# Order of the first chunk's exponentials, and place of the first w_o split, in a hybrid pooling and SSD decoder step

## The chip, the core and the metric

The kernel runs on one core of a Trainium2 chip. The core has five instruction queues that run side by side and meet only through semaphores: TensorE (PE, matrix products, its weight loads shown as PEld), VectorE (DVE), ScalarE (ACT), GpSimd (POOL) and SyncE (SP), which issues most of the DMA transfers. ACT issues the rest of them from its own queue, between its computations. Time is the device's time of one execution in microseconds (us); the metric is the median over executions.

## What is computed

One layer of a decoder on 1,024 prompt rows and 64 sample rows, together T = 1,088 columns in the kernel's transposed layout. The parts that matter here:

```
def layer(x, c, pos0, pool_buf, conv_buf, ssm_state, ...):
    h = rmsnorm(x, norm_g) * (1 + scale[:, None]) + shift[:, None]
    proj = h @ w_in
    u_pool, z_pool, z_ssm, xbc, dt_raw, g_raw = jnp.split(proj, SPLITS, axis=-1)
    ...
    p = (p * jax.nn.silu(z_pool)) @ w_pool_out
    ...
    y, ssm_new = ssd(xs, dt, A, Bm, Cm, ssm_state)
    y = rmsnorm(y * jax.nn.silu(z_ssm), ssm_norm_g)
    s = y @ w_ssm_out
    gates = jax.nn.sigmoid(g_raw)
    m = gates[..., :D_MODEL] * p + gates[..., D_MODEL:] * s
    x = x + gate[:, None] * (m @ w_o)

def step(h, inp):                      # inside ssd, one chunk of 128 rows
    acs = jnp.cumsum(dq * Ag, axis=1)
    decay = jnp.exp(jnp.where(mask, acs[:, :, None] - acs[:, None, :], -jnp.inf))
    cb = jnp.einsum('bign,bjgn->bijg', Cq, Bq)
    att = cb[..., None] * decay * dq[:, None]
    ...
```

All of it is float32. A product is made from three passes of a reduced format: each operand is split into a high part `hi` (a rounded copy, made by ACT) and a low part `lo = raw - hi` (a subtraction, made by POOL or DVE), and PE adds up hi·hi, hi·lo and lo·hi.

## The kernel before

The program has three stages that follow one another on PE.

**Projections (to about 827 us).** `h @ w_in` in pairs of column blocks, each by a seven-product scheme (`strassen`, L615). The last ten pairs (`run_units(light[-LAST:], 1, samples_beside)`, L1645) end in a sigmoid: for each half block, DVE adds the last product to a buffer (`s1`, `u2`, `u3`, `c2`; L625), ACT applies the sigmoid in place (`to_dram`, L721), and ACT issues the store to the scratch tensors `gp` and `gs` (L723). Beside each product a function `samples_beside` (L1596) counts steps in `due[0]` and issues other work at fixed steps. Work put under `with behind(engine)` (L406) stands in the scheduler's order right behind the last instruction of that engine written so far.

**Chunks (827 to about 1,124 us).** The SSD runs over 32 chunks (4 groups of 8) in a loop, L1768, with the products of `w_pool_out` and `w_ssm_out` between them (`products`, L1749, which run `gemm`, L354). In this stage the order on all five queues is as written: `in_line` (L340) ties every instruction to the one before it on its engine. For one chunk `i` the pieces are: `ch_load`, `d_load` and `z_load` (loads of `xb`, `dec` and `sz`); `ch_far` (from the second chunk of a group on ACT makes `cE = exp(-dec)`, L1402; then POOL masks `dec`, L1193); `ch_exps` (eight exponentials on ACT in place on `dec`, L1202); `ch_turn` (PE transposes `xb` into the PSUM tiles `pxs` and `pbs`, L118, and multiplies, L1415; ACT copies `bt`, L1417, and C, L1419); `ch_weigh` (DVE `xd`, `ps`, L1426 and L1427; ACT `xw`, L1429); `ch_skip` (ACT `xD`, L1435); `ch_mix` (DVE multiplies `dec`, L1439, and `cE`, L1441); `ch_lows` (DVE `btl`, L1444, and `xwl`, L1445); `ch_inner` (PE, L1214 to L1217 and L1462 to L1464). Chunk 0's `ch_far` and `ch_exps` do not stand in this loop: they are issued from `samples_beside`, at step `7 * LAST - 1`, before the last pair of sigmoids.

**Tail (1,131 us to the end).** Eight units `m` (`tail_unit`, L1898) make the last group's part of `s`, three column blocks each: DVE adds the earlier groups' sum to the product and multiplies by the row gate (L1882 and L1885 for `m = 0`; L1888 and L1890 for the others), POOL adds the pooling branch's part `mt` (L1886, L1892), `m_split` (L1851) makes `hi` on ACT (L1865) and `lo` on DVE (L1866) of the result, and `wo_split` (L1727) makes `hi` on ACT (L1729) and `lo` on POOL (L1730) of one block of 128 rows of `w_o`, which `wo_load` (L1723) has brought in. `m_split(m - 1)` is called in unit `m`. The product's PSUM tiles `mm` rotate over three buffers. The order is again as written on PE, DVE, ACT and POOL, while SP's order is left to the scheduler. At last come the products with `w_o` (L2000 to L2002), the norm and the stores.

Numbers at the end of a tile's name, as in `u_1850`, are those of one program's buffers; the profile leaves them out.

Of the kernel before, what the change touches and what calls it, by code (L numbers as in the profile page):

```python
# [21 lines left out]
D = 1024  # L22
# [24 lines left out]
def tile_pool_ssd_step(  # L47
# [9 lines left out]
    def nm(s):  # L57
        uid[0] += 1
        return f"{s}_{uid[0]}"
# [30 lines left out]
    def R(shape=(P, T), dt=F32):  # L90
        return hs.tile(list(shape), dt, tag="R", name=nm("R"), bufs=3)

    def Y4(pool, dt=F32R):
        return pool.tile([P, 4, T], dt, tag="Y", name=nm("Y"), bufs=2)

    def PB():
        return psB.tile([P, 512], F32, tag="ps", name=nm("ps"))
# [19 lines left out]
    def turn_r(out, src):  # L117
        nc.tensor.transpose(out.bitcast(F32R), src.bitcast(F32R), identR)  # L118
# [221 lines left out]
    def in_line(engines, begin=False):  # L340
        traced = nc.cur_bb.bb.instructions
        for i in traced[len(traced) if begin else line[0]:]:
            if i.engine in engines:
                if i.engine in line[1]:
                    tc.add_manual_dep(i, line[1][i.engine], mybir.DependencyInfo(
                        mybir.DependencyClass.NoSync, mybir.DependencyReason.DATA), reason="in_line")
                line[1][i.engine] = i.name
        line[0] = len(traced)
# [57 lines left out]
    def behind(engine, n=0):  # L406

        of = (i for i in reversed(nc.cur_bb.bb.instructions) if i.engine == engine)
        for _ in range(n):
            next(of)  # L410
        return tc.issue_after(next(of))
# [44 lines left out]
    def ready(d):  # L456
        def ws():
            with tc.high_priority(PRI):
                hi, lo = wtiles()
                load(hi.bitcast(F32), d[:, 0])  # L460
                load(lo.bitcast(F32), d[:, 1])
            return [(hi, lo)]
        return ws
# [726 lines left out]
    def far(dec, c):  # L1190

        if c < NC:
            nc.gpsimd.affine_select(dec, dec, [[0, 8], [1, P]], ALU.is_ge, FAR, base=0, channel_multiplier=-1)  # L1193
        else:
            dS = dec.rearrange("p h (b i) -> p h b i", i=8)
            nc.gpsimd.affine_select(dS, dS, [[0, 8], [8, NB], [1, 8]], ALU.is_ge, FAR, base=0, channel_multiplier=-1)
            nc.gpsimd.affine_select(dS, dS, [[0, 8], [-8, NB], [0, 8]], ALU.is_ge, FAR, base=0, channel_multiplier=1)

    def exps(dec, g, c):
        S = P if c < NC else NS  # L1200
        for h in range(8):
            act(dec[:, h], dec[:, h], AF.Exp, bias=acT[:S, c, 8 * g + h:8 * g + h + 1], scale=-1.0)  # L1202
# [160 lines left out]
    def ckt(shape, tag, bufs=2):  # L1363
        return (cl if tag in CKL else ca if tag in ("dec", "xb", "cE") else ck).tile(list(shape), F32, tag=tag, name=nm(tag), bufs=bufs)
# [19 lines left out]
    def ch_load(i):  # L1384
        g, c = divmod(i, NC)
        xbs[i] = ckt([P, 6, P], "xb", 3)
        load(xbs[i], xbc_d[g][:, :, c * P:c * P + P])

    def d_load(i):
        g, c = divmod(i, NC)  # L1390
        decs[i] = ckt([P, 8, P], "dec", 3)
        decays(decs[i], g, c)

    def z_load(i):
        g, c = divmod(i, NC)
        szs[i] = ckt([P, 4, P], "sz", 3)
        load(szs[i], z_d[g][:, :, c * P:c * P + P])

    def ch_far(i):
        if i % NC > 0:  # L1400
            cEs[i] = ckt([P, 8, P], "cE", 3)
            act(cEs[i], decs[i], AF.Exp, scale=-1.0)  # L1402
        far(decs[i], i % NC)

    def ch_exps(i):
        g, c = divmod(i, NC)
        exps(decs[i], g, c)

    def ch_turn(i):
        xb = xbs[i]  # L1410
        pxs[i], pbs[i] = PB(), PB()
        for q in range(4):
            turn_r(pxs[i][:, q * P:(q + 1) * P], xb[:, q])
        turn_r(pbs[i][:, :P], xb[:, 4])
        mm(pbs[i][:, P:2 * P], xb[:, 4], xb[:, 5], start=True, stop=True)  # L1415
        bts[i] = [ck.tile([P, P], F32R, tag=t, name=nm(t), bufs=2) for t in ("bt", "btl")]
        act(bts[i][0], pbs[i][:, :P], AF.Copy)  # L1417
        if i % NC > 0:
            act(pbs[i][:, 2 * P:3 * P], xb[:, 5], AF.Copy)  # L1419

    def ch_weigh(i):
        g, c = divmod(i, NC)
        heads = slice(8 * g, 8 * g + 8)
        pxv = pxs[i].rearrange("p (h d) -> p h d", d=64)
        xds[i] = ckt([P, 8, 64], "xd", 2)
        V.tensor_tensor(xds[i], pxv, dtT[:, c, heads].unsqueeze(2).to_broadcast([P, 8, 64]), ALU.mult)  # L1426
        V.tensor_tensor(pxv, pxv, wdT[:, c, heads].unsqueeze(2).to_broadcast([P, 8, 64]), ALU.mult)  # L1427
        xws[i] = [ck.tile([P, 512], F32R, tag=t, name=nm(t), bufs=2) for t in ("xw", "xwl")]
        act(xws[i][0], pxs[i], AF.Copy)  # L1429
# [166 lines left out]
    def samples_beside():  # L1596
        due[0] += 1
        if due[0] == 7 * LAST - 4:
            with behind(mybir.EngineType.SP):
                next(p_in)  # L1600
        if due[0] == 7 * LAST - 3:
            with behind(mybir.EngineType.SP):
                first_g.append(R())
                load(first_g[0], gp_d[0])
                first_ws[0] = ready(wp_d[0])()
        if due[0] == 7 * LAST - 2:
            next(p_in)
            with behind(mybir.EngineType.SP):
                ch_load(1)
                d_load(1)  # L1610
                first_ws[1] = ready(wp_d[1])()
                ch_load(2)
                d_load(2)
        if due[0] == 7 * LAST - 1:
            with behind(mybir.EngineType.Activation):
                ch_far(0)
                ch_exps(0)
        if due[0] == 7 * LAST:
            with behind(mybir.EngineType.DVE):
                next(p_in)  # L1620
        if due[0] <= FIRST:
            with behind(mybir.EngineType.DVE), behind(mybir.EngineType.Activation), behind(mybir.EngineType.PE):
                next(dt_steps[0], None)
            return
        while made_[0] < (due[0] - FIRST) * 4 * SSTEPS / (7 * LAST - FIRST - SPARE):
            made_[0] += 1
            if made_[0] == 4 * SSTEPS + 1:
                to_chunks()
            next(next(side, iter(())), None)
    SPARE = 7  # L1630

    def to_chunks():
        nonlocal right, ca
        right.__exit__(None, None, None)
        right = tc.tile_pool(name="ca", bufs=3, side="right", reuse_waits="tile")
        ca = right.__enter__()
        right_all.append(right)
        seq.append(0)
        ch_load(0)
        d_load(0)  # L1640
# [40 lines left out]
    def S_unit(g, m, done):  # L1681
        made_of = {}

        def piece(w, j):
            if not made_of:
                made_of[0] = done(m)
            gemm(w, [yh[g][:, q] for q in range(4)], [yl[g][:, q] for q in range(4)], 4, made_of[0], GB[j:j + 1])
        return (ready(ws_d[g][m]), piece)
# [34 lines left out]
    def wo_load(k, raw):  # L1723
        raws[k] = raw
        load(raw, w_o[0, k * P:(k + 1) * P, :])

    def wo_split(k, hi, lo, eng=None):  # L1727
        raw = raws.pop(k)
        act(hi, raw, AF.Copy)  # L1729
        (eng or nc.gpsimd).tensor_tensor(lo, raw, hi.bitcast(F32), ALU.subtract)  # L1730
        wo[k] = (hi, lo)
# [24 lines left out]
    ENGS = (mybir.EngineType.PE, mybir.EngineType.DVE, mybir.EngineType.Activation, mybir.EngineType.Pool, mybir.EngineType.SP,)  # L1756
    in_line(ENGS, True)
    z_load(0)
    ch_turn(0)
    ch_weigh(0)  # L1760
    ch_far(1)
# [85 lines left out]
    w4 = [Y4(hp), Y4(hp)]  # L1847
# [50 lines left out]
    def tail_unit(m):  # L1898
        pf, run_ = S_unit(3, m, m_done)

        def run(w):
            k = m + EARLY
            if k < 8:
                wo_load(k, M((P, D)))
            if 0 < m < 6:
                r_load(m + 2)
            run_(w, 0)
            if m == 0:
                run_(w, 1)
                run_(w, 2)  # L1910
            if m < 7:
                gains(m + 1)
            if m > 0:
                run_(w, 1)
                m_split(m - 1, M8 if m < 5 else G)
            if m < 4:
                wo_split(k, w4[0][:, m, :D], w4[1][:, m, :D])
            elif k < 8 and m < 6:
                wo_split(k, M((P, D), F32R), M((P, D), F32R))
            if m > 0:  # L1920
                run_(w, 2)
            if m > 1:
                samples[m - 2]()
        return (pf, run)
# [129 lines left out]
```

## Time and profile before

| quantity | us |
|---|---|
| three timed executions | 1292.78, 1290.96, 1286.81 |
| their median | 1290.96 |
| the profiled execution, as timed | 1292.2 |
| span of the profiled execution, first to last instruction | 1290.4 |
| PE busy in it | 1255.1 (97%) |
| DVE busy | 911.8 (71%) |
| ACT busy | 718.4 (56%) |
| POOL busy | 675.5 (52%) |
| mean granted TensorE clock | 0.995 of full speed |

A row of the timeline gives the start, the duration, the engine, the line, the operation, what is written from what, and in square brackets how long the engine had been idle before it and what released it. `ACTq` and `SPq` rows are DMA issues by those queues; they are not counted as busy. A row with `x8` merges eight like instructions. A row of the waits gives who waited, for whom, the total, the number of waits and the longest. A row of the windows gives a stretch, its length, and the busy time of the engine in it with the number of its instructions, then PEclk, the clock that TensorE was granted as a share of full speed, the DMA engines' busy share and GB/s.

### The profile page before, as it was taken

To read this page: it belongs to the slowest core of one execution; us is meant where nothing else is said; L and a number is where in the kernel's file an instruction comes from. 1 tells how busy PE (TensorE), PEld (TensorE's weight loads), DVE (VectorE), ACT (ScalarE), POOL (GpSimd) and SP (SyncE) were. 2 spreads that over 40 slices of the span, in tenths; PEclk is the share of its full clock that TensorE was granted. 3 is DMA by queue.
4 is the path that set the end of the run, shared out by engine and by line. 5 is a ranking of instruction groups with operands and counts; after the bars stand their busy time and mean duration, and the time that the engine had idled before them with its cause. 6 is when DMAs were issued, how large, how long until landed. Compare 5 with 4: busy or idle time off the path is not lost. (4 is left out here: it accounts for less than half of the span.)

```text
span 1290.4 us, 26363 instructions
## 1 busy us (share of the span) xinstructions
PE 1255.1 (97%) x9771; PEld 1176.8 (91%) x9771; DVE 911.8 (71%) x1584; ACT 718.4 (56%) x1685; POOL 675.5 (52%) x555
## 2 busy tenths in 40 slices
PE   7999999999999999999999999999999999999997
PEld 6779999989999999999889999989999999989786
DVE  4686778865979588776667665488667879767533
ACT  4665356465556655554554564686887768522211
POOL 1007658678869777564344443446465656636000
PEclk9999999999999999999999999999999999999999
DMA  9736354465456453444546555889666666575431
GB/s 329 243 116 220 117 164 160 143 198 178 142 164 219 144 184 126 152 154 121 160 134 202 168 155 157 288 289 317 221 197 184 185 215 207 161 270 181 158 105 50
DMA packets 225730, 234.90 MB, mean 182 GB/s; under 512 B 30370, under 2 KB 177010, under 8 KB 225595
## 3 DMA queue, kind: packets, MB, share of 16 engines
q1 hardware_dynamic: 155808, 159.01, 39.6%
q10 hardware_dynamic: 69794, 74.22, 16.8%
q8 instruction: 77, 1.26, 0.4%
q14 instruction: 51, 0.41, 0.1%
HBM read 158.67 MB, written 74.62 MB: 181 GB/s over the span
## 5 line engine op out<-in xcount | busy, mean ns | idle before, releaser
L169 POOL TENSOR_TENSOR wlo<-rawA,whi 128x512 fp32r<-128x512 f32 x120 | 186.8, 1561 | 186.6 <-ACT whi L166 102.0
L169 POOL TENSOR_TENSOR wlo<-raw,whi 128x512 fp32r<-128x512 f32 x92 | 149.4, 1631 | 125.1 <-ACT whi L166 120.7
L360 PE MATMUL mm<-Y,whi 128*128 128x352 f32 (+1 forms) x480 | 160.0, 333 | 2.7 <-DVE G L1890 2.5
L361 PE MATMUL mm<-Y,whi 128*128 128x352 f32 (+1 forms) x480 | 157.8, 329 | 0.4 <-DVE Y L1516 0.4
L362 PE MATMUL mm<-Y,wlo 128*128 128x352 f32 (+1 forms) x480 | 157.3, 328 | 0.0
L611 PE MATMUL mm<-Y,wlo 128*128 128x272 f32 x496 | 143.7, 290 | 4.1 <-POOL wlo L169 3.6
L609 PE MATMUL mm<-Y,whi 128*128 128x272 f32 x496 | 146.4, 295 | 0.3 <-ACT whi L166 0.2
L609 PE MATMUL ps<-Y,whi 128*128 128x272 f32 x496 | 144.4, 291 | 2.2 <-ACT o L809 1.6
L610 PE MATMUL ps<-Y,whi 128*128 128x272 f32 x496 | 143.1, 289 | 0.0
L610 PE MATMUL mm<-Y,whi 128*128 128x272 f32 x496 | 142.8, 288 | 0.0
L611 PE MATMUL ps<-Y,wlo 128*128 128x272 f32 x496 | 142.6, 288 | 0.0
L166 ACT ACTIVATE whi<-rawA 128x512 fp32r<-128x512 f32 x125 | 78.0, 626 | 97.9 <-PE ps L610 43.2
L1057 DVE SCALAR_TENSOR_TENSOR GA<-GA,cvT,GA 128x1112 f32<-128x1112 f32 x72 | 126.4, 1758 | 0.3
L166 ACT ACTIVATE whi<-raw 128x512 fp32r<-128x512 f32 x96 | 58.8, 626 | 90.7 <-DVE raw L555 39.3
L611 PEld LDWEIGHTS mm<-Y,wlo 128*128 128x128 f32 x496 | 93.4, 188 | 6.0 <-POOL wlo L169 4.9
L609 PEld LDWEIGHTS ps<-Y,whi 128*128 128x128 f32 x496 | 93.3, 188 | 3.7 <-ACT o L809 1.8
L360 PEld LDWEIGHTS mm<-Y,whi 128*128 128x128 f32 x480 | 90.6, 189 | 5.5 <-DVE G L1890 3.5
L609 PEld LDWEIGHTS mm<-Y,whi 128*128 128x128 f32 x496 | 93.3, 188 | 2.4 <-ACT whi L166 0.9
L610 PEld LDWEIGHTS mm<-Y,whi 128*128 128x128 f32 x496 | 93.4, 188 | 0.7 <-issue 0.6
L610 PEld LDWEIGHTS ps<-Y,whi 128*128 128x128 f32 x496 | 93.3, 188 | 0.3 <-issue 0.2
L611 PEld LDWEIGHTS ps<-Y,wlo 128*128 128x128 f32 x496 | 93.5, 188 | 0.2 <-issue 0.2
L361 PEld LDWEIGHTS mm<-Y,whi 128*128 128x128 f32 x480 | 90.5, 189 | 2.6 <-DVE Y L1516 0.9
(459 smaller groups left out, 3842.8 us busy)
## 6 DMA issues: line engine op xcount, KB each, us to landing
rawA<-in_w_in SPq DMA_DIRECT2D x46, 512.0 KB
dec<-acs_d SPq DMA_DIRECT2D x32, 512.0 KB
xbc<-GA ACTq DMA_DIRECT2D x24, 512.0 KB
xb<-xbc SPq DMA_DIRECT2D x32, 384.0 KB
rawA<-in_w_in SPq DMA_DIRECT2D x32, 256.0 KB
pw<-in_w_ssm_out ACTq DMA_DIRECT2D x32, 256.0 KB
ws<-ph ACTq DMA_DIRECT2D x32, 256.0 KB
ws<-pw SPq DMA_DIRECT2D x32, 256.0 KB
```

Of the source, the lines that this page charges most:

```text
L166: ins = act(hi[:, :, :ncols], raw[:, :, :ncols], AF.Copy)
L169: (eng or nc.gpsimd).tensor_tensor(lo[:, :, :ncols], raw[:, :, :ncols], hi[:, :, :ncols].bitcast(F32), ALU.subtract)
L360: mm(ps[:, :n], a, rh[k][:, o:o + n], start=(k == 0), stop=False)
L361: mm(ps[:, :n], a, rl[k][:, o:o + n], start=False, stop=False)
L362: mm(ps[:, :n], b, rh[k][:, o:o + n], start=False, stop=(k == nk - 1))
L609: mm(p, hi, ah, start=(k == 0), stop=False)
L610: mm(p, hi, al, start=False, stop=False)
L611: mm(p, lo, ah, start=False, stop=(k == 3))
L1057: V.scalar_tensor_tensor(d[:, :n], rp[:, k:k + n], cvT[:, 24 * k + mc:24 * k + mc + 1], d[:, :n], ALU.mult, ALU.add)
```

## The change

Three edits in the text of the program:

```diff
@@ samples_beside, L1614
         if due[0] == 7 * LAST - 1:
-            with behind(mybir.EngineType.Activation):
-                ch_far(0)
-                ch_exps(0)
+            ch_far(0)
@@ before the chunk loop, L1757
     in_line(ENGS, True)
     z_load(0)
+    with behind(mybir.EngineType.Activation):
+        ch_exps(0)
     ch_turn(0)
@@ tail_unit, L1907
             run_(w, 0)
             if m == 0:
+                wo_split(k, w4[0][:, m, :D], w4[1][:, m, :D])
                 run_(w, 1)
                 run_(w, 2)
@@ tail_unit, L1916
-            if m < 4:
+            if 0 < m < 4:
                 wo_split(k, w4[0][:, m, :D], w4[1][:, m, :D])
-            elif k < 8 and m < 6:
+            elif m and k < 8 and m < 6:
                 wo_split(k, M((P, D), F32R), M((P, D), F32R))
```

On ACT, at the seam between the projections and the chunks: `u_1851` and `u_1850` are the buffers of the last two sigmoid blocks, `gs_147` and `gs_148` their stores' targets, `dec_10994` is chunk 0's decay tile, `bt`, `xw` and `xb` belong to chunk 0, `cE` and `dec_11134` to chunk 1.

```order
 L721 ACTIVATE u_1851_10958<-u_1851_10958 128x272 x2
 L723 DMA gs_147<-u_1851_10958 128x544
+L721 ACTIVATE u_1850_10957<-u_1850_10957 128x272 x2
+L723 DMA gs_148<-u_1850_10957 128x544
 L1202 ACT_TABLE_LOAD
 L1202 ACTIVATE dec_10994<-dec_10994,acT 128x128 x8
-L721 ACT_TABLE_LOAD
-L721 ACTIVATE u_1850_10957<-u_1850_10957 128x272 x2
-L723 DMA gs_148<-u_1850_10957 128x544
 L1417 ACTIVATE bt_11239<-ps_11232 128x128
 L1429 ACTIVATE xw_11245<-ps_11231 128x512
-L1402 ACT_TABLE_LOAD
```

The last block's two sigmoids and its store stand ahead of the eight exponentials, and two of three loads of ACT's function table are no longer in the program. No other instruction of ACT has moved.

On POOL, at the start of the tail: `m_15315` and `m_15375` are the raw `w_o` blocks 0 and 1, `Y_15304` holds the low parts, `G_12282` is the sum of unit 0 and `m_15317` its `mt`.

```order
+L1728 TENSOR_TENSOR Y_15304<-m_15315,Y_15303 128x1024
 L1886 TENSOR_TENSOR G_12282<-G_12282,m_15317 128x1088
-L1730 TENSOR_TENSOR Y_15304<-m_15315,Y_15303 128x1024
-L1730 TENSOR_TENSOR Y_15304<-m_15375,Y_15303 128x1024
+L1728 TENSOR_TENSOR Y_15304<-m_15375,Y_15303 128x1024
 L1892 TENSOR_TENSOR G_12356<-G_12356,m_15379 128x1088
```

The low part of `w_o` block 0 stands ahead of unit 0's addition instead of behind it (the line has the number 1728 in the changed file). The order on ACT, DVE and PE is as before in this place.

On SP, in the same place: `m_15519` is the `mt` of unit 3 and `m_15587` the raw `w_o` block 4.

```order
+L1876 DMA m_15519<-m_160 128x1088
 L460 DMA whi_15511<-ws_213 128x512
 L461 DMA wlo_15512<-ws_213 128x512
-L1735 DMA R_15377<-gs_144 128x1088
+L1733 DMA R_15377<-gs_144 128x1088
 L460 DMA whi_15583<-ws_214 128x512
-L1876 DMA m_15519<-m_160 128x1088
+L1723 DMA m_15587<-in_w_o 128x1024
 L461 DMA wlo_15584<-ws_214 128x512
-L1725 DMA m_15587<-in_w_o 128x1024
```

The load of unit 3's `mt` has moved ahead of four transfers, and that of `w_o` block 4 ahead of one.

## The prediction

> **What bounds the kernel now.** I read the windows first, to see which engine is full in the two stages that are touched, then PE's waits from 812 us on, then the timeline around each wait.
>
> ```profile
> 860.00:880.00 20.00, 20.00 (x165) 18.91 (x164) 17.46 (x29) 15.48 (x43) 11.40 (x13) 1.00 0.91 310
> ...
> PE mm L360 <- DVE G L1890: 2.5, 1, 2.5
> PE ps L118 <- DVE btl L1444: 2.1, 1, 2.1
> PE ps L1214 <- DVE dec L1439: 0.6, 1, 0.6
> PE mm L361 <- DVE Y L1516: 0.4, 1, 0.4
> ```
>
> The first row gives busy times in the order PE, PEld, DVE, ACT, POOL: PE is full for all 20 us in the chunks, and the four waits below it, 5.6 us together, are all that it loses to another engine behind 812. So PE sets the end, and the change can bring only what shortens a wait or raises PE's clock, and cost only what makes a new wait. The two long waits lie where the two edits are. The first, at the second chunk, is led up to by these rows of ACT, DVE and PE:
>
> ```profile
> 825.65 0.75 ACT L721 ACTIVATE u<-u 128x272 f32<-128x272 f32 x2 [2.63 <-DMA wlo<-wp]
> 827.23 0.33 ACTq L723 DMA_DIRECT2D gs<-u  x1
> 827.64 1.28 ACT L1202 ACT_TABLE_LOAD   x1 [1.24 <-DMA xb<-xbc]
> 828.93 2.45 ACT L1202 ACTIVATE dec<-dec,acT 128x128 f32<-128x128 f32 x8
> 831.40 1.28 ACT L721 ACT_TABLE_LOAD   x1
> 832.69 0.75 ACT L721 ACTIVATE u<-u 128x272 f32<-128x272 f32 x2
> 833.48 0.33 ACTq L723 DMA_DIRECT2D gs<-u  x1
> 833.90 0.28 ACT L1417 ACTIVATE bt<-ps 128x128 fp32r<-128x128 f32 x1 [0.46 <-ACT u L721]
> 834.69 1.28 ACT L1402 ACT_TABLE_LOAD   x1
> 840.88 0.28 ACT L1419 ACTIVATE ps<-xb 128x128 f32<-128x128 f32 x1
> ...
> 826.95 0.44 DVE L625 TENSOR_TENSOR u<-u,ps 128x272 f32<-128x272 f32 x1 [1.07 <-PE ps L611]
> 834.27 1.22 DVE L1439 TENSOR_TENSOR dec<-dec,ps 128x1024 f32<-128x1024 f32 x1 [3.16 <-issue]
> 838.30 0.51 DVE L1670 TENSOR_TENSOR R<-mm,R 128x352 f32<-128x352 f32 x1
> 841.27 1.22 DVE L1439 TENSOR_TENSOR dec<-dec,ps 128x1024 f32<-128x1024 f32 x1 [2.46 <-ACT ps L1419]
> ...
> 843.97 0.25 PE L118 MATMUL ps<-identR,xb 128*128 128x128 f32 x1 [2.13 <-DVE btl L1444]
> ```
>
> Read backwards: PE (843.97) waits for `btl`, which follows L1439 of chunk 1 (841.27) on DVE; that had waited 2.46 us for ACT's L1419 (840.88). From `bt` (833.90) to there ACT never pauses: 6.98 us of work, 1.28 of it a table load. So ACT is what is late, and what it does before 840.88 comes off PE's wait one for one.
>
> **Edit 1, the exponentials behind the last sigmoids.** Removed: the load at 831.40 and the load at 834.69, because the sigmoids stand together and the exponential table is still in place for `cE`. Moved: two sigmoids and their store, ahead of load and exponentials.
>
> New times: the sigmoids' input is ready at 826.95 + 0.44 = 827.39, so they start at 827.64 in the load's place and end at 828.39. The store's issue takes 0.33 and has followed its sigmoids by 0.04 (833.44 to 833.48) or 0.83 (826.40 to 827.23); with the load (1.28) and the exponentials (2.45) behind it they end between 832.5 and 833.3. `bt` of chunk 0 stands next. It started at 833.90, right behind the store's issue at 833.48 + 0.33; I don't see in these rows all that it needs, so its bounds are 832.6 and 833.9, and I take the middle, 833.25, 0.65 earlier. From there to L1419 the stretch is 1.28 shorter. Gain at DVE's L1439: 0.65 + 1.28 = **1.93** [1.28 to 2.58]. DVE itself is ready by 838.30 + 0.51 = 838.81, more than 2 us before, so it doesn't bind. PE's wait falls from 2.13 to 0.2, and PE gains 1.9; at the upper bound the wait is used up at 2.13, and only the small one of 0.6 on chunk 0's L1439 can add to it. What is queued behind the later exponentials on ACT is `bt`, `xw`, `cE`, `xD` and chunk 1's exponentials; DVE's two L1439 wait for these, and PE for DVE: this is where a loss would show.
>
> A page of the Trainium skill, "ScalarE: Activation LUTs", section "What ACT_TABLE_LOAD costs", puts a switch at about 1283 ns of load plus about 1380 ns of drain. By it two loads would be worth 5.3 us instead of 2.6, an estimate, and the wait at PE would be gone altogether. The rows do not agree on the second part: the load at 831.40 ends at 832.68 and the sigmoid starts at 832.69.
>
> **The clock behind that wait.** These are PE's windows around both waits: length, PE busy, PEclk, DMA share, GB/s.
>
> ```profile
> 841.62:845.03 3.41, 1.28 (x11) 1.00 0.95 261
> 845.03:848.44 3.41, 3.41 (x19) 0.50 1.08 356
> ...
> 1148.82:1152.23 3.41, 2.59 (x15) 1.00 0.94 289
> 1152.23:1155.64 3.41, 1.72 (x11) 1.00 0.51 168
> ```
>
> After a window with 1.28 us of work PE ran one window at half speed; work that takes 3.41 there takes 1.71 at full speed, so the wait cost another **1.7**. With 0.2 us of idle time left this falls away. The tail's wait lies across an edge between two windows, 2.59 and 1.72 busy, and no half clock followed; all in one window, it would leave 0.9 busy, less than 1.28. So the same wait costs 1.7 or nothing by where the edge falls, which a single profile can't promise. Bounds of this term: 0 and 1.7.
>
> "TensorE: Matmul & The Clock Gate" in the Trainium skill, section "What's actually happening", has the windows free-running and the clock drop after at least one idle window of about 3.4 us. Taken as a wholly idle window, it would put this term at 0, since 2.13 us of waiting is too short; the measured 0.50 after a window that was not wholly idle decides against that reading. The free-running edge agrees with the two waits' different outcomes.
>
> **Edit 2, the first w_o split inside unit 0.** Rows of POOL, DVE, ACT and PE:
>
> ```profile
> 1144.53 2.54 POOL L1886 TENSOR_TENSOR G<-G,m 128x1088 f32<-128x1088 f32 x1 [20.08 <-DVE G L1885]
> 1147.02 4.76 POOL L1730 TENSOR_TENSOR Y<-m,Y 128x1024 fp32r<-128x1024 f32 x2
> 1153.94 2.55 POOL L1892 TENSOR_TENSOR G<-G,m 128x1088 f32<-128x1088 f32 x1 [2.16 <-DVE G L1890]
> 1161.21 2.55 POOL L1892 TENSOR_TENSOR G<-G,m 128x1088 f32<-128x1088 f32 x1
> ...
> 1149.09 0.44 DVE L1855 TENSOR_TENSOR sh<-G,sh 128x64 fp32r<-128x64 f32 x1
> 1149.45 3.42 DVE L1866 TENSOR_TENSOR m<-G,m 128x1024 fp32r<-128x1024 f32 x1
> 1157.17 0.21 DVE L1855 TENSOR_TENSOR sh<-G,sh 128x64 fp32r<-128x64 f32 x1
> 1157.76 1.23 DVE L1866 TENSOR_TENSOR m<-G,m 128x1024 fp32r<-128x1024 f32 x1 [0.38 <-ACT m L1865]
> ...
> 1136.64 1.06 ACT L1729 ACTIVATE Y<-m 128x1024 fp32r<-128x1024 f32 x1 [0.55 <-DMA m<-in_w_o]
> 1148.22 1.04 ACT L1729 ACTIVATE Y<-m 128x1024 fp32r<-128x1024 f32 x1
> ...
> 1153.92 0.43 PE L360 MATMUL mm<-Y,whi 128*128 128x352 f32 x1 [2.50 <-DVE G L1890]
> 1155.95 1.09 PE L1860 MATMUL ps<-Y,sh 128*128 128x512 f32 x4
> 1162.79 0.39 PE L1860 MATMUL ps<-Y,sh 128*128 128x512 f32 x1
> ```
>
> DVE's L1866 takes 3.42 us instead of 1.23, and ends 1.09 behind POOL's second L1730 (1151.78), about its own length: it stood still while POOL ran. PE follows its end (1152.87) by 1.05.
>
> After: the low part of block 0 has its input from 1137.70 (ACT) and runs in POOL's idle 20 us, done by about 1140.2, so the 2.4 us moved ahead of L1886 have 4.3 us of cover; without that cover unit 0's sum would come up to 2.4 later. The second L1730 then waits for ACT's L1729, 1148.22 + 1.04 = 1149.26, and can start at about 1149.34. DVE's L1855 starts at 1149.09 and now takes 0.21, so L1866 starts at 1149.25 to 1149.30, first by 0.04 to 0.1 us. L1866 ends at about 1150.5, PE can go on at 1151.55 instead of 1153.92, and POOL's L1730, held until 1150.4, ends at 1152.75 instead of L1892 starting at 1153.94: that is 1.2 earlier.
>
> Whoever starts first keeping the path for its whole instruction is also the rule of the Trainium skill, "SBUF — State Buffer", section "SBUF: two separate sides", and by it DVE would block POOL here; if POOL's start came first, edit 2 would bring nothing.
>
> Not all of PE's 2.4 reaches the end. PE goes round a unit in 1162.79 - 1155.95 = 6.84 us, POOL's L1892 in 1161.21 - 1153.94 = 7.27, so PE catches up with the sums, and already waits for them here, on the chain that ended last:
>
> ```profile
> 1178.49 1.05 ACT G L1865
> 1179.56 1.23 DVE G L1866
> ...
> 1181.85 0.43 PE mm L360
> ```
>
> From 1181.85 on the end is set through POOL's L1892, which comes 1.2 earlier. I take **1.2** [0 to 2.4]. SP's moved loads I cost at nothing: they are issues in a stretch in which POOL idles 20 us and PE has no wait; without that cover each transfer put ahead of another would delay it by an issue, 0.33 us in ACT's rows, so four of them 1.3.
>
> **Sum:** 1.9 + 1.7 + 1.2 = 4.8, so the profiled execution, 1292.2 as timed, would become 1287.4. It lies 1.24 above the median of the runs shown, and against that median the forecast is 1290.96 - 4.8 = **1286.1**.
>
> **Rivals.**
> - *The tail's wait also costs a clock window in the timed runs.* The windows above show that 0.9 us busy would do it; part of it is taken back at 1181.85, so 1.4 more: 1284.7.
> - *The half-clock window isn't in the runs that make the median.* For it: the edge of the windows decides, and the three times differ by 6 us. Then 1.7 is missing: 1287.8.
> - *POOL takes the path first.* The margin is under 0.1 us, and in the rows of before POOL's second L1730 won against L1866 right behind L1855. Then 1.2 is missing: 1287.4.
> - *The start gains nothing.* The last store is held on ACT's queue, as ACT was held 2.63 us ahead of 825.65. A hold of h moves the exponentials and `bt` by h, so the gain there is 2.58 - h, nothing at 2.6; only edit 2 is left: 1289.8.
> - *Slower.* The same place, held longer: everything of chunks 0 and 1 on ACT now stands behind that store's issue, where the exponentials used to run ahead of it. From h = 3.8 on it eats edit 2's gain too; at h = 6 the start loses 3.4, and the kernel stands at 1290.96 + 3.4 - 1.2 = 1293.2. Against it: the issue before had a gap of 0.83 at most.
> - *No effect:* both waits are replaced by others of the same length, 1291.
>
> **How the numbers follow.** Chances: forecast 0.33, tail's clock window 0.22, no window in the median 0.11, POOL first 0.18, start without gain 0.08, slower 0.06, none 0.02. A difference under 0.5% (6.5 us) can't be told from no change here: faster means below 1284.5, slower above 1297.4. Below 1284.5 lie nearly half of the second case, some of the first where both gains reach their upper bounds (2.1 + 1.7 + 2.4 = 6.2), together 0.22; above 1297.4 only a store held some 10 us or something unseen, 0.04; the rest is 0.74. The range runs from both upper bounds with a clock window in the tail, less a little (1282), to the case in which only part of edit 2 is left, 1291; the slower one and the far end of the fast ones are left out.
>
> **What would show it.** Right: ACT's seam with one load and the sigmoids' 0.75 ahead of it; `bt` near 833.2; the second L118 wait under 0.9 and no window at 0.50 near 845; L1866 at 1.23 near 1149.3 and L1892 near 1152.7. Wrong: an idle gap on ACT ahead of the last store or of `bt`; L1866 still at 3.4; a new wait on L1214 for chunk 0's `dec`, or on a tile of `whi` behind the moved loads.

## The result and the profile after

The changed kernel takes 1284.65 us (median of 22 runs) against 1288.62 us for the kernel before (22 runs): ratio 0.9965, 95% interval 0.9956 to 0.9974, or 4.5 us less (3.4 to 5.7). One of its 22 runs took 2019.72 us, at a mean granted clock of 0.558; it is counted in the median and left out of the ratio. The two medians lie 4.0 us apart, inside the interval. The profiled execution was timed at 1287.48 us, 4.7 less than that of before. In microseconds the kernel before was 2.3 below the median of three runs that the prediction started from.

PE's waits behind 805 us (who waited, for whom, total, number of waits, longest):

```profile
PE ps L118 <- DVE btl L1444: 0.7, 1, 0.7
PE ps L1214 <- DVE dec L1439: 0.5, 1, 0.5
PE mm L361 <- DVE Y L1516: 0.4, 1, 0.4
```

The 2.1 us wait at the second chunk is down to 0.7, and the 2.5 us wait in the tail is gone. The seam on ACT, with DVE's last L625 addition and its L1439 of chunk 1 below (start, duration, engine, line, operation):

```profile
827.22 0.33 ACTq L723 DMA_DIRECT2D gs<-u  x1
827.65 0.75 ACT L721 ACTIVATE u<-u 128x272 f32<-128x272 f32 x2 [1.15 <-DMA xb<-xbc]
828.52 0.33 ACTq L723 DMA_DIRECT2D gs<-u  x1
828.93 1.28 ACT L1202 ACT_TABLE_LOAD   x1 [0.54 <-DMA whi<-wp]
830.23 2.45 ACT L1202 ACTIVATE dec<-dec,acT 128x128 f32<-128x128 f32 x8
833.16 0.28 ACT L1417 ACTIVATE bt<-ps 128x128 fp32r<-128x128 f32 x1 [0.48 <-DMA gs<-u]
833.82 1.06 ACT L1402 ACTIVATE cE<-dec 128x1024 f32<-128x1024 f32 x1
838.72 0.28 ACT L1419 ACTIVATE ps<-xb 128x128 f32<-128x128 f32 x1
...
826.29 0.44 DVE L625 TENSOR_TENSOR u<-u,ps 128x272 f32<-128x272 f32 x1 [1.07 <-PE ps L611]
839.10 1.22 DVE L1439 TENSOR_TENSOR dec<-dec,ps 128x1024 f32<-128x1024 f32 x1 [1.03 <-ACT ps L1419]
```

One load of the table is left, ahead of the exponentials, and `cE` follows without one. But `bt` now stands 0.48 us idle behind them, put down to a store of sigmoids. Already the addition (826.29) comes 0.66 ahead of before (826.95): the projections, which the change doesn't touch, took that much less in this execution. From here on moments are counted from the start of that addition.

The clock: PE's windows of 3.41 us around the wait (PE busy, PEclk, DMA share, GB/s) are all at full speed.

```profile
841.28:844.69 3.41, 2.88 (x23) 1.00 1.01 356
844.69:848.11 3.42, 3.42 (x38) 1.00 1.11 344
```

The tail, on POOL and DVE:

```profile
1134.14 2.37 POOL L1728 TENSOR_TENSOR Y<-m,Y 128x1024 fp32r<-128x1024 f32 x1 [13.39 <-PE ps L1844]
1140.82 2.55 POOL L1886 TENSOR_TENSOR G<-G,m 128x1088 f32<-128x1088 f32 x1 [4.31 <-DVE G L1885]
1145.64 3.35 POOL L1728 TENSOR_TENSOR Y<-m,Y 128x1024 fp32r<-128x1024 f32 x1 [2.27 <-DMA whi<-ws]
1148.95 2.55 POOL L1892 TENSOR_TENSOR G<-G,m 128x1088 f32<-128x1088 f32 x1
1153.77 2.49 POOL L1728 TENSOR_TENSOR Y<-m,Y 128x1024 fp32r<-128x1024 f32 x1 [2.27 <-ACT Y L1727]
1156.22 2.55 POOL L1892 TENSOR_TENSOR G<-G,m 128x1088 f32<-128x1088 f32 x1
...
1145.51 1.22 DVE L1866 TENSOR_TENSOR m<-G,m 128x1024 fp32r<-128x1024 f32 x1
```

PE on the chain that ended last:

```profile
1176.86 0.43 PE mm L360
```

DVE's L1866 starts 0.13 us ahead of POOL's second low part and takes 1.22 us; now it is POOL that stands still, 3.35 us instead of 2.4. Behind it the sums L1892 go round in 1156.22 - 1148.95 = 7.27 us, the period that they had before.

Where the time went is seen from the start of the same matmuls of PE (before; after):

| PE's matmul | before, from the addition | after | difference |
|---|---|---|---|
| the L118 that waits for `btl` (the last of chunk 2) | 17.01 | 15.51 | -1.50 |
| 50 matmuls on | 23.66 | 20.61 | -3.05 |
| last one ahead of the tail's wait | 324.14 | 321.10 | -3.04 |
| first one behind the tail's wait | 326.96 | 321.50 | -5.46 |
| L360 on the last chain (1181.85; 1176.86) | 354.89 | 350.56 | -4.33 |
| end of the span | 463.50 | 459.42 | -4.08 |

So 1.50 came at the wait for `btl`, 1.55 from the half-speed window, and 2.42 at the tail's wait, of which 1.13 was given back by 1176.86; 0.25 went behind that, and 0.66 came by chance from the projections.

### The profile page after: what moved, and what is told of

It is laid out like the page before. It is cut to its first block, busy times and chain, and to the rows that moved or that the text cites. A ratio compares the mean times of both kernels' runs of the same rounds, so it can differ in the third digit from the quotient of the medians.

```text
span 1285.7 us, 26359 instructions
## 1 busy us (share of the span) xinstructions
PE 1254.3 (98%) x9771; PEld 1175.2 (91%) x9771; DVE 907.9 (71%) x1584; ACT 716.0 (56%) x1683; POOL 675.9 (53%) x555
## 5 line engine op out<-in xcount | busy, mean ns | idle before, releaser
L360 PE MATMUL mm<-Y,whi 128*128 128x352 f32 (+1 forms) x480 | 159.8, 333 | 0.7
L361 PE MATMUL mm<-Y,whi 128*128 128x352 f32 (+1 forms) x480 | 157.3, 328 | 0.4 <-DVE Y L1516 0.4
L362 PE MATMUL mm<-Y,wlo 128*128 128x352 f32 (+1 forms) x480 | 156.8, 327 | 0.0
L360 PEld LDWEIGHTS mm<-Y,whi 128*128 128x128 f32 x480 | 90.3, 188 | 4.2 <-DVE G L1890 2.4
L361 PEld LDWEIGHTS mm<-Y,whi 128*128 128x128 f32 x480 | 90.2, 188 | 2.6 <-DVE Y L1516 0.9
```

The costliest lines, as they stand in the source:

```text
L360: mm(ps[:, :n], a, rh[k][:, o:o + n], start=(k == 0), stop=False)
L361: mm(ps[:, :n], a, rl[k][:, o:o + n], start=False, stop=False)
L362: mm(ps[:, :n], b, rh[k][:, o:o + n], start=False, stop=(k == nk - 1))
```

## The experiments

All kernels are compared by that same count where a profile tells more than the times: the projections alone differ by up to 8 us from one profiled execution to the next (the addition starts at 828.38 in `only_tail` and at 820.36 in `bt_elsewhere`, with the same program ahead of it). A part of this is the clock: in the projections the first of these two profiles has two windows at 0.50, at 56 and 671 us, and the second has none. `pool_halves`, `table_back`, `pad32` and `table_back2` were run once each, for the profile.

**Each edit alone.** `only_start` has the first part of the diff, `only_tail` the second:

```diff
 only_start: as the changed kernel, but in tail_unit
-                wo_split(k, w4[0][:, m, :D], w4[1][:, m, :D])
                 run_(w, 1)
 only_tail: as the kernel before, but in tail_unit
+                wo_split(k, w4[0][:, m, :D], w4[1][:, m, :D])
                 run_(w, 1)
```

> Edit 1 alone, the tail as before. Theory (ACT is late at the second chunk): the wait of L118 for btl falls from 2.1 to about 0.7 us, no window at 0.50 behind it, and the PE work in front of the tail runs about 3.0 us earlier than before, counted from the last L625 addition; the tail's 2.5 us wait and DVE's 3.42 us L1866 are still there, so that 3 us is also the gain at the end: ratio about 0.9975. Rival (the whole gain comes from the tail): ratio 1.000. Rival (the two edits need each other): the start's gain is lost in the tail, and the wait there grows by it.

Ratio 0.9985 (0.9971 to 0.9999). PE's waits, then two of its windows ahead of the tail:

```profile
PE mm L360 <- DVE G L1890: 2.5, 1, 2.5
PE ps L118 <- DVE btl L1444: 0.6, 1, 0.6
```

```profile
1121.14:1124.55 3.41, 3.41 (x28) 1.00 0.65 161
1124.55:1127.97 3.42, 3.42 (x13) 0.50 0.86 296
```

The start's gain comes without edit 2: 50 matmuls behind L118, PE is 3.77 us ahead of before, where some 3.0 were expected, and the tail's wait is untouched. Of this 1.6 us went in a half-speed window at 1124.55, behind a window in which the profile shows PE full; no other kernel here has a window at 0.50 there. At the end 1.7 us are left (461.79 against 463.50 from the addition). The times agree with that: 1.9 us less (0.1 to 3.7), where the expectation was 3.2. So the two edits don't need each other, and a half-speed window can turn up where no wait is.

> Edit 2 alone, the chunk start as before. Theory: L1866 of unit 0 takes 1.23 us, PE's 2.5 us wait for L1890 is gone, of which 1.0 to 1.2 us reaches the end, because POOL's sums go round in 7.27 us against PE's 6.84; the 2.1 us wait of L118 and, depending on where the clock's windows fall, a half-speed window remain. Ratio 0.999 (0.998 if the tail's wait cost half-speed windows in the timed runs of before). Rival (all 2.4 us reach the end): 0.998 without any clock effect, and PE's later waits for L1890 don't grow. Rival (POOL first): L1866 stays at 3.4 us, ratio 1.000.

Ratio 0.9989 (0.9976 to 1.0002). PE's wait at the start, its windows there, and DVE and POOL in the tail:

```profile
PE ps L118 <- DVE btl L1444: 2.1, 1, 2.1
```

```profile
841.35:844.77 3.42, 1.64 (x13) 1.00 0.91 301
844.77:848.18 3.41, 3.04 (x27) 1.00 0.96 301
```

```profile
1148.84 1.22 DVE L1866 TENSOR_TENSOR m<-G,m 128x1024 fp32r<-128x1024 f32 x1
1148.98 3.35 POOL L1730 TENSOR_TENSOR Y<-m,Y 128x1024 fp32r<-128x1024 f32 x1 [2.27 <-ACT Y L1729]
```

DVE is first again, by 0.14 us. Against before, PE is 1.81 us ahead at the chunks (no half-speed window this time, though the wait is the same) and 3.11 ahead at the L360 of the last chain: edit 2 brings 1.3 us, not the 2.4 that its wait held. The times alone don't show this gain, since their interval reaches past 1.000; the trace does.

**The second low part in two pieces**, in the kernel before, to see what makes DVE stand still:

```diff
     def wo_split(k, hi, lo, eng=None):
-        (eng or nc.gpsimd).tensor_tensor(lo, raw, hi.bitcast(F32), ALU.subtract)
+        for o in (0, 512):
+            c = slice(o, o + 512)
+            (eng or nc.gpsimd).tensor_tensor(lo[:, c], raw[:, c], hi[:, c].bitcast(F32), ALU.subtract)
```

> The kernel before, with every low part of w_o made by POOL in two instructions of 512 columns. Theory (whichever engine starts first keeps the path for one whole instruction, the other stands still): DVE's L1866 of unit 0 gets in behind the first half of POOL's second block, takes about 2.3 to 2.4 us instead of 3.42, POOL's second half waits for it, and PE's wait for L1890 falls from 2.5 to about 1.4 us. Rival (the two share the bandwidth of one path): L1866 keeps its 3.4 us, since POOL moves the same bytes. Rival (POOL takes precedence over a waiting DVE): L1866 again waits for both halves, 3.4 us or more.

DVE's line (L1868 and L1892 here are L1866 and L1890 of before), PE's wait in the tail, and its windows at the start:

```profile
1145.84 2.32 DVE L1868 TENSOR_TENSOR m<-G,m 128x1024 fp32r<-128x1024 f32 x1
```

```profile
PE mm L360 <- DVE G L1892: 1.9, 2, 1.6
```

```profile
837.05:840.47 3.42, 1.29 (x11) 1.00 0.94 283
840.47:843.88 3.41, 3.41 (x14) 0.50 0.95 330
```

2.32 us: a wait for the one half of POOL's that had started before it, and its own 1.23; and PE's longest wait ahead of an L360 fell to 1.6. With the same bytes moved by POOL, sharing a bandwidth would have left 3.4. So the path is held for one instruction at a time, and an instruction that waits gets it at the next boundary. That agrees with the Trainium skill, "SBUF — State Buffer", section "SBUF: two separate sides", which calls the pair of ports an exclusive lock.

**The table loads put back** into the changed kernel, by a sigmoid of 128x8 elements behind the exponentials; `table_back` gives it a buffer of its own, `table_back2` one that the kernel has already, and `pad32` has the buffer and its memset but no sigmoid:

```diff
     with behind(mybir.EngineType.Activation):
         ch_exps(0)
+    with behind(mybir.EngineType.Activation):
+        act(ch_dummy, ch_dummy, AF.Sigmoid)
     ch_turn(0)
```

> The changed kernel with a sigmoid of 128x8 elements behind the first chunk's exponentials, which brings back the two loads of the function table, and nothing else. Theory (a load costs its 1.28 us on ACT and no more, and ACT is what is late): bt about 1.0 us later and L1439 of chunk 1 2.3 us later than in the changed kernel, counted from the last L625 addition; PE's waits there (0.5 at L1214 and 0.7 at L118) grow by 2.3 us together, and by 1.7 more where a window at 0.50 follows. Rival (a switch also costs a drain of 1.38 us): 5.1 us later. Rival (another engine is late too): less than 2 us later.

ACT's rows and DVE's L1439 of chunk 1:

```profile
828.62 2.45 ACT L1202 ACTIVATE dec<-dec,acT 128x128 f32<-128x128 f32 x8
831.10 1.28 ACT L1762 ACT_TABLE_LOAD   x1
832.39 0.21 ACT L1762 ACTIVATE dmy<-dmy 128x8 f32<-128x8 f32 x1
832.51 0.26 ACT L1417 ACTIVATE bt<-ps 128x128 fp32r<-128x128 f32 x1
833.27 1.28 ACT L1402 ACT_TABLE_LOAD   x1
839.86 1.22 DVE L1439 TENSOR_TENSOR dec<-dec,ps 128x1024 f32<-128x1024 f32 x1 [2.46 <-ACT ps L1419]
```

L1439 of chunk 1 starts 14.44 us behind the addition, against 12.10 in the second profile of the changed kernel, whose ACT rows up to the exponentials lie at the same moments: 2.34 later, and PE's two waits are 0.7 (L1214) and 2.1 (L118). Of the 2.34, `bt` accounts for 0.92, because the first load and the sigmoid fill the 0.51 us that `bt` stood idle in that profile; the other 1.4 come with the second load. So far the loads' own price. But the end came 4.6 us later than in that profile (463.01 against 458.42), and the rest grew evenly through the chunk stage, without a wait. That was left to two more kernels.

> The changed kernel with one more buffer of 32 bytes in each partition and DVE's memset of it, no sigmoid and no load of a table. In the kernel with the sigmoid put back PE lost 2 us more through the chunk stage, its 384-column products taking 339 to 341 ns instead of 336 to 338, with no wait and a granted clock of 1.00. Theory (the buffer's place in memory, which moves the tiles behind it by 32 bytes, makes PE's products slower): the same products take 339 to 341 ns here too, and the time from the last L625 addition to the end is 2 us above the 458.4 to 459.4 us of the changed kernel's two profiles. Rival (chance, or the later start of the chunks): 336 to 338 ns and 458.4 to 459.4 us.

PE's 384-column products from 860 to 1120 us (busy us, mean ns, idle), first `pad32`, then the changed kernel:

```profile
L360 PE MATMUL mm<-Y,whi 128*128 128x384 f32 x108 | 36.8, 341 | 0.0
L361 PE MATMUL mm<-Y,whi 128*128 128x384 f32 x108 | 36.6, 339 | 0.0
```

```profile
L360 PE MATMUL mm<-Y,whi 128*128 128x384 f32 x108 | 36.5, 338 | 0.0
L361 PE MATMUL mm<-Y,whi 128*128 128x384 f32 x108 | 36.3, 336 | 0.0
```

Without any sigmoid the products are slower by 0.9% at the same clock, and the end comes at 460.59, 2.2 later than 458.42. So it is the buffer, and not its memset, which `table_back2` below has too without being slower. These products are not all of it: with L362 beside L360 and L361, the 324 of this width hold 1.0 us more than in the changed kernel.

> The sigmoid behind the first chunk's exponentials again, its buffer now taken from those that the kernel has already, so that nothing moves in memory. Theory of the loads (1.28 us each): L1439 of chunk 1 starts 14.4 us behind the last L625 addition instead of 12.1, and the end comes 2.2 to 2.3 us later than in the changed kernel (460.7 to 461.7 us behind that addition), 1.7 more if a window at 0.50 follows the wait. Theory of the buffer's place: the 384-column products of the chunk stage take 336 to 338 ns. Rival (the later start slows the products): 339 to 341 ns and 463 us.

The end comes at 460.85, 2.4 behind 458.42; L1439 of chunk 1 starts at 14.47, and the products take 338 and 336 ns. PE's waits:

```profile
PE ps L118 <- DVE btl L1444: 2.1, 1, 2.1
PE ps L1214 <- DVE dec L1439: 0.7, 1, 0.7
```

The emptiest window around the L118 wait, first of `table_back`, then of `table_back2`; neither was followed by one at 0.50:

```profile
841.46:844.88 3.42, 2.33 (x15) 1.00 0.95 299
837.32:840.73 3.41, 1.87 (x14) 1.00 1.06 278
```

Each load costs its 1.28 us on ACT, and both come through to the end, less the half microsecond that `bt` had stood idle. The drain of some 1.38 us that the Trainium skill, "ScalarE: Activation LUTs", section "What ACT_TABLE_LOAD costs", adds to each would have made 5 us of it; it isn't there.

**The first `bt` elsewhere**, to find what the 0.48 us were:

```diff
         bts[i] = [ck.tile([P, P], F32R, tag=t, name=nm(t), bufs=2) for t in ("bt", "btl")]
+        if i == 0:
+            bts[i][0] = sm.tile([P, P], F32R, tag="stc", name=nm("bt"), bufs=4)
```

> The changed kernel, with the first bt tile in other memory. In the changed kernel this copy stood idle 0.48 us behind the exponentials, put down to the landing of a store of sigmoids. Theory (the wait is for memory: bt lies over a sigmoid buffer that is still being stored): bt follows the exponentials within 0.1 us, DVE's L1439 and L1419 come 0.4 to 0.5 us earlier, and PE's wait for btl falls from 0.7 to about 0.25 us; the time falls by 0.45 us, under what the rounds can tell. Rival (the wait is for something else, as the products in PSUM or a later tile of the same pool): the gap of 0.48 us stays, ahead of bt or of xw.

Ratio 0.9951 (0.9935 to 0.9967). ACT behind the exponentials, and all that PE waits behind 805:

```profile
823.44 2.46 ACT L1202 ACTIVATE dec<-dec,acT 128x128 f32<-128x128 f32 x8
825.80 0.26 ACT L1419 ACTIVATE bt<-ps 128x128 fp32r<-128x128 f32 x1
```

```profile
PE mm L361 <- DVE Y L1518: 0.4, 1, 0.4
```

The gap is gone, and with it both waits of PE at the chunks. The wait was for the memory that `bt` took over from a sigmoid block, whose store had not landed. The changed kernel's second profile puts the same idle time, 0.51 us, down to PE's L1415; but `both_more`, whose sigmoids lie at the same moments, has none of it, and `bt` is the only thing moved there at the start. More than 0.48 was gained (1.8 us from the addition to the end, against the first profile of the changed kernel), because the ACT queue was also held less ahead of the last sigmoids in this execution; in `both_more` below, where those lie as in the changed kernel's second profile, L1439 of chunk 1 comes 0.63 earlier.

**Two blocks of w_o in unit 0**, to find what gives back 1.1 us in the tail:

```diff
         def run(w):
             k = m + EARLY
-            if k < 8:
+            if k < 8 and m != 1:
                 wo_load(k, M((P, D)))
+            if m == 0:
+                wo_load(1, M((P, D)))
...
             if m == 0:
-                wo_split(k, w4[0][:, m, :D], w4[1][:, m, :D])
+                for q in range(2):
+                    wo_split(q, w4[0][:, q, :D], w4[1][:, q, :D])
```

(Unit 1 then makes no split.)

> The changed kernel, with the split of w_o block 1 in unit 0 too, behind that of block 0: POOL does it between 1136.8 and 1139.3, in the 4.3 us that it still idles ahead of unit 0's sum. Theory (POOL's chain of sums sets the end in units 2 to 5, and its start is delayed by block 1's low part): unit 1's L1892 starts right behind DVE's L1890, about 1.15 us earlier against the units before it, and PE's later waits for L1890 shrink by 1.1 us in all; ratio to before 0.9957 where the changed kernel had 0.9965. Rival (the raw block lands too late and POOL holds up L1886): unit 0's sum later, PE waits again ahead of block 2 of unit 1, slower than the changed kernel by 1 us or more. Rival (DVE or ACT sets the period, not POOL): no gain.

Ratio 0.9956 (0.9943 to 0.9968). POOL:

```profile
1129.70 4.75 POOL L1728 TENSOR_TENSOR Y<-m,Y 128x1024 fp32r<-128x1024 f32 x2 [13.44 <-ACT Y L1727]
1136.28 2.56 POOL L1886 TENSOR_TENSOR G<-G,m 128x1088 f32<-128x1088 f32 x1 [1.83 <-DVE G L1885]
1143.27 2.56 POOL L1892 TENSOR_TENSOR G<-G,m 128x1088 f32<-128x1088 f32 x1 [4.43 <-DVE G L1890]
```

Unit 1's L1892 now waits for DVE, not for a low part. The sums go on at 7.27 us a round, but from an earlier start. PE was 4.55 us ahead of the changed kernel where the tail's wait had been, most of it by chance in the projections, and is 5.69 ahead at the L360 of the last chain: 1.14 us, as much as the 1.13 that had been given back. The chain of POOL's sums was what took the tail's gain back. (At the end of the span it is 5.95: the 0.25 that the changed kernel lost behind the last chain, by the table above, is not lost here.)

Why a round takes 7.27 us is seen on ACT, in the changed kernel:

```profile
1151.53 0.26 ACT L1854 ACTIVATE sh<-G 128x64 fp32r<-128x64 f32 x1 [5.97 <-POOL G L1892]
1151.70 1.04 ACT L1865 ACTIVATE m<-G 128x1024 fp32r<-128x1024 f32 x1
1152.64 1.05 ACT L1727 ACTIVATE Y<-m 128x1024 fp32r<-128x1024 f32 x1
```

The round is a loop through two engines: ACT waits for POOL's sum, makes the sum's `hi` and only then that of the next `w_o` block, and POOL idles 2.27 us until it has the latter (1153.77). With L1727 ahead of L1854, in ACT's idle time, POOL's own 2.49 + 2.55 = 5.04 us would be left, less than PE's 6.84. That is an estimate; no run tried it, and the raw block would have to be there by then.

**Both of these**, beside the changed kernel on one chip:

> The changed kernel itself, beside the next one on the same chip. All theories: ratio to before 0.9965 as in the result, within 0.0015; the waits of 0.7 (L118) and 0.5 us (L1214) at the first chunks as in its profile; every difference of its profile ahead of the last L625 addition is chance.

> The changed kernel with the first bt tile in other memory and with the split of w_o block 1 in unit 0. Theory (the two gains lie at different waits and add up): 1.2 us at the first two chunks and 1.35 us in the tail against the changed kernel, ratio to before 0.9945; PE's waits behind 812 us shrink to the 0.4 us at L361 and under 0.2 us in the tail. Rival (the start's gain is eaten by the chain of sums in the tail): only 1.35 us, ratio 0.9955.

The changed kernel had 0.9962 (0.9945 to 0.9979), `both_more` 0.9953 (0.9938 to 0.9969). The changed kernel's waits at the first chunks were not quite those of its first profile: 0.6 us at L118, and none at L1214. From the addition to the end the profiles give 458.42 and 456.92 us, 1.5 less, where the theory had 2.55. Behind the waits of the start PE is 0.65 us ahead, at the end of the chunks 0.46, and at the L360 of the last chain 1.59. So the tail brings 1.13, near to the 1.35 expected, and the start much less than its 1.2. The total lies near to the rival's 1.35, but not for its reason: the tail did not eat the start's gain, which was small before it got there. Both kernels beat the one before; that `both_more` beats the changed one is shown by its profile, where PE keeps only the 0.4 us at L361, and not by the times, whose intervals overlap.

## Why the prediction was right

The forecast was 4.8 us less, the measurement 4.5 (3.4 to 5.7). The mechanism is as stated, but for how often the half-speed window follows the wait. By its steps:

- **ACT is late at the second chunk, and what is taken off it comes off PE's wait (1.9, bounds 1.28 to 2.58).** Right in kind, and on average in size: L1439 of chunk 1 came 1.50 us earlier in the first profile of the changed kernel and 2.21 in the second, and 2.22, 1.93 and 2.26 in `only_start`, `two_ahead` and `pad32`, which have the same start: 2.0 in the mean. The term is a middle that one execution can't fix. What moves it is what the prediction left open, a hold of the stores on ACT's queue and what `bt` needs: the last sigmoids start 1.35 or 0.58 us behind the addition, and `bt` waits for the landing of a store until its memory is free. The rival with a hold of 2.6 us or more was not seen.
- **The half-speed window (1.7).** Measured 1.55 in this pair of profiles, but too sure as a term of the median: of five profiles with the wait of 2.1 us, two (before, `pool_halves`) have a window at 0.50 behind it and three (`only_tail`, `table_back`, `table_back2`) don't. Averaged it is nearer to 0.7. That the edge of the windows decides had been stated as the rival at 1287.8, and the traces bear it out: in the first two the wait leaves 1.28 and 1.29 us of work in one window, in the other three it is shared out so that the emptier window holds 1.64 (`only_tail`), 2.33 (`table_back`) and 1.87 (`table_back2`). The granted clocks of the timed runs give a second count. Their mean is 0.9970 over the 47 runs of the five kernels with edit 1 that were timed beside the one before (`only_start`, `bt_elsewhere`, `two_ahead`, `after_again`, `both_more`), and 0.9961 over the 58 runs of `only_tail` and the kernel before on the same two chips. A window of 3.41 us at half clock takes 0.0013 off the mean of a run of 1,286 us. So the first have some 0.7 such windows fewer (0.3 to 1.0), an estimate, worth about 1.1 us; where in the run they lie the clocks don't say. The truth lies between that rival and the forecast.
- **A window in the tail too** (the heaviest rival): not seen behind the 2.5 us wait in either profile that has it, before and `only_start`.
- **DVE first on the path, by 0.04 to 0.1 us.** Right: 0.13 and 0.14, and the price of standing still passed to POOL.
- **1.2 of the tail's 2.4 us reaches the end.** Right: 1.29 in the first pair of profiles, 1.30 with edit 2 alone, for the reason stated, the 7.27 us round of POOL's sums; `two_ahead` shows it by starting the round earlier.
- **SP's moved loads at nothing.** Right: none of PE's waits is for a weight tile.

With the start at 2.0, the window at 0.7 to 1.1 and the tail at 1.3 the sum would have been 4.0 to 4.4, also inside the measured interval; the times don't tell these sums from 4.8. So that 4.8 lies so near to 4.5 is partly luck: the window's term was 0.6 to 1.0 us too large, which the total alone doesn't show.

## What to carry to other kernels

Functions that need another table on the same engine are grouped first, where the grouped work doesn't have to wait for a store or its memory: each load saved was worth its 1.28 us because that engine was late, less the half microsecond for which `bt` then waited for a store. Where two engines share a path, look at which of two instructions starts first, and by how much: here 0.13 us decides 2.4 us of another engine's wait. And ask of a wait that disappears which other round follows behind it: the next one here took back half of the gain, and starting it earlier was enough to have it again.

## What was not expected

- A buffer of 32 bytes per partition that nobody waits for made 384-column products 339 to 341 ns instead of 336 to 338 at a granted clock of 1.00, and the kernel 2.2 us longer, in both kernels that have it (`table_back` and `pad32`). Which tile's address matters was not tried.
- The same wait of PE was followed by a window at 0.50 in two profiles of five, and one such window stood behind a window that the profile shows full. Each profile's half-speed windows fix the grid of 3.41 us on which the windows lie. On it, in the twelve profiles of this case, from 30 us to the last products, all 11 windows with at most 1.40 us of PE work (the profile's modelled ends) were followed by one at 0.50; between 1.64 and 1.76 us 7 were and 4 were not; from 1.78 us on none was, but for the one full window of `only_start`. What decides it there is open.
